# Down as seven products of halves over its first 2048 rows, the other 768 rows plain and late

## The chip, the cores and the metric

The kernel runs on one core of one Trainium2 chip. Its time is the device time of one execution in microseconds (us), and the median over several executions is what is compared. A core has five engines with queues of their own: TensorE (PE in the profile, PEld for its weight loads), VectorE (DVE), ScalarE (ACT), GpSimd (POOL) and SyncE (SP), which here only issues transfers. Transfers are also issued from POOL's queue, among them those that add what they load to what the buffer holds.

## The reference

Two layers of an encoder over 512 tokens and 1024 columns, in float32. Each layer mixes the tokens (attention, pooling and a gated chunk mixing, not touched here) and then applies a SwiGLU block. What the change touches is the last line of the loop:

```python
for l in range(DEPTH):                                   # 2
    ...
    x = x + jnp.einsum('bsn,nd->bsd', mix, w_o[l])
    h = rmsnorm(x, ffn_norm[l])
    g = jnp.einsum('bsd,df->bsf', h, w_gate[l])          # 1024 -> 2816
    u = jnp.einsum('bsd,df->bsf', h, w_up[l])
    x = x + jnp.einsum('bsf,fd->bsd', jax.nn.silu(g) * u, w_down[l])   # 2816 -> 1024: Down
return rmsnorm(x, final_norm)
```

## The kernel before

**Precision.** Each matmul operand is split into two float32r parts, high and low, and a product is three matmuls: high by high, high by low, low by high (`mm3`, line 533; `mm`, line 1243). The high part is a copy on ScalarE, the low part a subtraction on VectorE (or on GpSimd where the engine is `nc.either`). For weights this is `split` (line 560): it writes a `wu` tile of 128 x 2 x 1024, of which there are three. `weights` (line 568) loads a unit of 128 x 1024 into one of two `raw` buffers and splits it. For activations the halves are called `xp`.

**Buffers.** Most things lie in one pool of 32 tiles `u` of 4 KB a partition (`NU`, line 68): activations (`ac`), their halves (`xp`), sums (`xs`), the gated values (`mg`), and the weights of the seven-product stages (`wr`). PSUM has eight banks in three groups, s (3), p (3) and b (2). `anybank` rotates over all of them, `bank("b")` takes one of the two b banks.

**Order.** Nothing is issued where the code stands. `Program` (lines 288 to 490) records every operation, lays out an order by a list scheduler with its own costs, gives out the buffers and then issues all of it from line 488; so every row of the profile names L488, and tiles are told apart by name. An operation that opens a new buffer may be placed at most `lead` matmuls ahead of TensorE (100 in the SwiGLU block, line 1165).

**Gate and up.** They are done as seven products of halves already (Strassen's scheme): tokens, rows and columns are cut in two, and the seven products of sums of quarters are accumulated in six banks, three regions z, y and x of two banks each (`region_banks`, line 1237). The order of the products is 1, 5, 6, 3, 7, 2, 4. The sums of weight quarters are made on VectorE (products 5 and 6 add to a running tile `chain`) or by an adding transfer on POOL's queue (products 7 and 4). The 1408 columns of each half are done in three chunks of 512, 512 and 384 (index c). `consume` (line 1264) turns each result into silu(g) times u and transposes it into `ac` tiles.

**Down in layer 0** (line 1363). A plain product with the weights standing still: 8 output blocks m of 128 columns, each over 22 row blocks k of 128 with all 512 tokens moving, three matmuls each. All 22 halves of the activations (`part`, line 1349) are needed for block 0 already. The result has columns in the partitions, as the residual `res` has; it is added to `res`, scaled into layer 1's input (`scaled`, line 619) and squared for the norm (`squares`, line 629).

**Down in layer 1** (line 1375). The residual is transposed to token rows first (32 transposes). Then the activations stand still: 22 row blocks k, four token tiles, two column halves, into all eight banks; the last three row blocks are kept back, so that the token tiles are finished one after the other, with the final norm and the output.

## Time and profile before

| | |
|---|---|
| median of three runs | 1126.03 us (1125.56 to 1127.54) |
| the profiled execution | 1125.68 us |
| its span, from the first to the last instruction | 1123.8 us |
| mean granted clock of TensorE | 0.991 |
| busy: PE, DVE, ACT, POOL | 1091.9, 781.6, 604.6, 167.9 us |
| Down in layer 0, on TensorE | 440.9 to 562.8 us |
| Down in layer 1, on TensorE | 993.4 to 1113.6 us |

How to read it: a matmul's row in the timeline has the start in us, the length, the operation with output and inputs, and in brackets how long the engine stood idle before it and whose end released it. Matmuls overlap, so a length is longer than the step from one to the next. In a table by windows the columns are busy time and number of instructions of PE, PEld, DVE, ACT and POOL, then the granted clock (1.00 is full speed), the share of the transfer engines' time and GB/s. In a list of groups the two numbers behind the bar are busy time and the mean of one in ns, then idle time before them and who ended it.

### The profile page before, as it was taken

How to read it: one execution, taken by the hardware profiler on the slowest of the kernel's cores; microseconds unless marked ns; L12 is line 12 of the kernel's file. 1: busy time of each engine (PE TensorE's matmuls, PEld its weight loads, DVE VectorE, ACT ScalarE, POOL GpSimd, SP SyncE). 2: the span in 40 equal slices, each digit the busy share in tenths (PEclk: the TensorE clock that was granted, in tenths of full speed). 3: DMA queues.
4: the chain of work that ended last, by engine and by line, in shares of the span. 5: the costliest groups of instructions: out<-in, count | busy, mean ns of one | idle time of the engine just before them, and what ended most of it. 6: DMA issues, size and time to landing. Idle time of an engine off the chain costs nothing.

```text
span 1123.8 us, 14427 instructions
## 1 busy us (share of the span) xinstructions
PE 1091.9 (97%) x5388; PEld 920.2 (82%) x5388; DVE 781.6 (70%) x1107; ACT 604.6 (54%) x949; POOL 167.9 (15%) x187
## 2 busy tenths in 40 slices
PE   9999899999999988999999999999999999999996
PEld 7787788888888987888888877888888889978885
DVE  7679996997786769333336898959976877743324
ACT  6367774775565556222233687747655646642223
POOL 0217320100100111000001363202001100110001
PEclk9999999999999998999999999999999999999998
DMA  6332215456744661333332322165656645533331
GB/s 208 99 117 76 62 57 209 110 148 153 180 101 122 140 151 50 101 94 94 109 101 67 116 62 66 55 241 117 167 167 131 130 119 117 122 94 94 94 113 75
DMA packets 40933, 130.10 MB, mean 116 GB/s; under 512 B 5360, under 2 KB 5616, under 8 KB 40864
## 3 DMA queue, kind: packets, MB, share of 16 engines
q1 hardware_dynamic: 32784, 103.85, 28.7%
q0 software_dynamic: 7504, 24.29, 13.0%
q8 instruction: 42, 0.69, 0.3%
q10 hardware_dynamic: 576, 1.05, 0.2%
q14 instruction: 27, 0.22, 0.1%
HBM read 122.74 MB, written 2.23 MB: 111 GB/s over the span
## 4 chain that ended last, share of the span: by engine, by line
PE 82%; DVE 9%; issue 4%; ACT 3%; POOL 1%; DMA 1%; POOLq 0%; ACTq 0%; DVEq 0%
PE ps L488 82%; DVE u L488 3%; DVE t L488 2%; DVE s L488 1%; DVE wu L488 1%; ACT u L488 1%; ACT t L488 1%; DVE mg L488 1%; ACT wu L488 1%; DVE xp L488 1%; DMA wr<-in_wts 0%; DVE vz L488 0%; DMA u<-u 0%; POOL s L488 0%; ACT vm L488 0%
## 5 line engine op out<-in xcount | busy, mean ns | idle before, releaser
L488 PE MATMUL ps<-wu,xp 128*128 128x512 f32 (+1 forms) x2544 | 555.9, 377 | 3.3 <-ACT wu L488 2.9
L488 PEld LDWEIGHTS ps<-wu,xp 128*128 128x128 f32 x2544 | 466.1, 188 | 76.7 <-ACT wu L488 3.4
L488 DVE TENSOR_TENSOR wu<-wr,wu 128x1024 fp32r<-128x1024 f32 (+1 forms) x168 | 190.4, 1134 | 84.6 <-ACT wu L488 83.7
L488 ACT ACTIVATE wu<-wr 128x1024 fp32r<-128x1024 f32 (+1 forms) x168 | 166.3, 990 | 135.8 <-PE ps L488 109.9
L488 PE MATMUL ps<-u,wu 128*128 128x512 f32 x972 | 236.1, 395 | 2.3 <-DVE wu L488 1.7
L488 PEld LDWEIGHTS ps<-u,wu 128*128 128x128 f32 x972 | 178.9, 188 | 41.8 <-DVE wu L488 3.0
L488 DVE TENSOR_TENSOR wu<-raw,wu 128x1024 fp32r<-128x1024 f32 (+1 forms) x88 | 101.9, 1160 | 153.8 <-ACT wu L488 153.3
L488 ACT ACTIVATE wu<-raw 128x1024 fp32r<-128x1024 f32 (+3 forms) x98 | 97.2, 994 | 201.1 <-PE ps L488 153.2
L488 PE MATMUL ps<-xp,wu 128*128 128x512 f32 x528 | 122.1, 394 | 0.2 <-ACT ac L488 0.2
L488 PEld LDWEIGHTS ps<-xp,wu 128*128 128x128 f32 x528 | 100.6, 191 | 21.7 <-ACT ac L488 0.7
L488 PE MATMUL ps<-u,u 128*128 128x256 f32 (+3 forms) x516 | 107.9, 346 | 4.2 <-ACT t L488 2.6
L488 POOL DMA_DIRECT2D wr<-in_wts x48 | 41.9, 873 | 425.5 <-DVE wr L488 233.4
L488 PEld LDWEIGHTS ps<-u,u 128*128 128x128 f32 (+2 forms) x516 | 75.5, 188 | 18.1 <-ACT t L488 4.2
L488 ACT COPY t<-ps 128x512 f32<-128x512 f32 (+3 forms) x114 | 56.3, 495 | 34.3 <-PE ps L488 30.9
L488 DVE TENSOR_TENSOR u<-ps,u 128x512 fp32r<-128x512 f32 (+1 forms) x104 | 70.0, 684 | 6.1 <-ACT u L488 5.0
L488 ACT ACTIVATE u<-ps 128x512 fp32r<-128x512 f32 (+1 forms) x104 | 61.2, 596 | 16.0 <-PE ps L488 14.7
L488 DVE TENSOR_TENSOR wr<-wr,wr 128x1024 f32<-128x1024 f32 (+1 forms) x48 | 53.9, 1131 | 5.6 <-DMA wr<-in_wts 5.3
L488 ACT ACTIVATE t<-ps,s 128x512 f32<-128x512 f32 x64 | 43.7, 687 | 9.4 <-DVE s L488 7.8
L488 POOL TENSOR_SCALAR t<-t,s 128x512 f32<-128x512 f32 x54 | 37.6, 702 | 66.2 <-DVE s L488 49.7
L488 DVE TENSOR_TENSOR t<-ps,t 64x256 f32<-64x256 f32 (+2 forms) x80 | 42.2, 548 | 5.2 <-ACT t L488 4.8
L488 DVE TENSOR_TENSOR res<-ps,res 128x512 f32<-128x512 f32 x40 | 27.5, 688 | 25.3 <-PE ps L488 25.1
L488 DVE TENSOR_REDUCE s<-ps 128x1 f32<-128x512 f32 x64 | 42.4, 679 | 0.8 <-PE ps L488 0.6
(128 smaller groups left out, 845.3 us busy)
## 6 DMA issues: line engine op xcount, KB each, us to landing
raw<-in_wts SPq DMA_DIRECT2D x82, 512.0 KB, 3.5
wr<-in_wts SPq DMA_DIRECT2D x64, 512.0 KB, 4.8
wr<-in_wts POOLq DMA_DIRECT2D x32, 512.0 KB, 5.6
wr<-in_wts SPq DMA_DIRECT2D x32, 384.0 KB, 3.4
wr<-in_wts POOLq DMA_DIRECT2D x16, 384.0 KB, 5.5
u<-u SPq DMA_DIRECT2D x32, 128.0 KB, 2.3
raw<-in_wts SPq DMA_DIRECT2D x8, 320.0 KB, 3.0
res<-in_xT SPq DMA_DIRECT2D x8, 256.0 KB, 5.2
```

Source lines behind the costliest of these rows:

```text
L488: getattr(getattr(nc, op.engine), op.method)(*[real(x) for x in op.args], **{k: real(x) for k, x in op.kw.items()})
```

## The change

Down of both layers becomes one piece of code. Its first 16 row blocks (those of chunks 0 and 1, eight of each half of F) are done as seven products of halves: two halves of the tokens, two halves of the rows, two halves of the columns. The last six row blocks (chunk 2) are done plainly (`rest`), once for each half of the columns, and late: for columns 512 to 1023 between products 7 and 4, for columns 0 to 511 after product 4. The order is product 1, product 5, products 6 and 3 block by block in turn, 2, 7, late part 1, 4, late part 0. The weights are packed to match (34 loads of 512 KB for a layer instead of 22, eight of them adding transfers); `consume` now transposes each token tile of chunks 0 and 1 by itself, into tiles by quarter. In layer 0, too, the result now has tokens in the partitions: `back` transposes it, 32 transposes in all, and adds it to `res`. Since columns 512 to 1023 are finished first, layer 1 takes its input blocks in the order 4 to 7, 0 to 3. The splits of the products' weights name VectorE, those of the late part leave the engine open.

The core of the diff:

```diff
-        KORDER = range(KD)
+        KORDER = range(KD) if l == 0 else (4, 5, 6, 7, 0, 1, 2, 3)
...
-        if not last:
...
-                for k in range(KF):
...
-                    xh, xl = part(k)
-                    mm3(ps[:], w[:, 0, s], w[:, 1, s], xh, xl, k == 0, k == KF - 1)
+        def back(y, t, s):
+            ps = bank("b")
+            for m in range(4):
+                nc.tensor.transpose(ps[:, m * P : (m + 1) * P], y[:, m * P : (m + 1) * P], ident[:])
+            nc.vector.tensor_tensor(out=rows(t, s), in0=cols4(ps[:]), in1=rows(t, s), op=ALU.add)
...
+        def halved(src):
+            hi, lo = (upool.tile([P, 4, HALF], F32R, tag="u", name=nm("xp"), bufs=NU) for _ in range(2))
+            nc.scalar.activation(flat(hi), flat(src), AF.Copy)
+            add(flat(lo), flat(src), f32(flat(hi)), ALU.subtract)
+            return hi, lo
...
+            if p == 5:
+                sums[c] = upool.tile([P, 4, HALF], F32, tag="u", name=nm("xs"), bufs=NU)
+                add(flat(sums[c]), flat(x21), flat(x22), ALU.subtract)
+                add(flat(x21), flat(x11), flat(x21), ALU.subtract)
+            elif p == 6:
+                add(flat(sums[c]), flat(sums[c]), flat(x11), ALU.subtract)
+            else:
+                add(flat(sums[c]), flat(sums[c]), flat(x12))
...
+            if p == 1:
+                chain[b] = fetch(l, dn_unit(0, 0, b))
+                return chain[b]
+            if p == 2:
+                return fetch(l, dn_unit(1, 0, b))
+            if p == 4:
+                add_loaded(l, chain[b], dn_unit(1, 0, b))
+                return chain[b]
+            if p == 7:
+                raw = fetch(l, dn_unit(0, 1, b))
+                add_loaded(l, raw, dn_unit(1, 1, b))
+                return raw
+            if p == 3:
+                return chain["22"]
+            raw = fetch(l, dn_unit(0, 1, b) if p == 5 else dn_unit(1, 1, b))
+            chain["22"] = raw
+            add(chain[b][:], chain[b][:], raw[:])
+            return chain[b]
...
+        def products(ps_):
+            xs = {}
+            for b in range(4):
+                for p in ps_:
+                    if b % 2 == 0:
+                        xs[p] = halved(sum_of(p, b // 2))
+                    xh, xl = xs[p]
+                    wu = split(operand(p, b), U, nc.vector)
+                    for j in range(2):
+                        for kk in range(2):
...
+        def rest(h, targets, after):
+            wus = [weights(l, dn_unit(2, h, b)) for b in range(3)]
+            for i, (banks, opens) in enumerate(targets):
+                for j in range(2):
+                    for k in range(6):
...
+        products([1])
...
+        products([5])
...
+        products([6, 3])
...
+        products([2])
+        products([7])
+        spare = [bank("b"), bank("b")]
...
+        rest(1, [(reg["y"], False), (spare, True)], after1)
+        products([4])
+        if not last:
+            next_inputs(1)
...
+        rest(0, [(reg["x"], False), (reg["z"], False)], after0)
+        if not last:
+            next_inputs(0)
+            xg = nxt
```

Where the instructions come to stand is shown at three places. The first is TensorE's queue at the end of up in layer 0. Before, the last up product (128x384) is followed by the transposes of the gated values `mg` of chunk 2, and then by the first matmuls of Down (`ps_4088`, output block 0):

```order
L488 MATMUL ps_3759<-wu_3984,xp_2454 128x384
L488 MATMUL ps_3759<-wu_3984,xp_2333 128x384 x2
L488 MATMUL ps_3759<-wu_3984,xp_2454 128x384
L488 MATMUL ps_4058<-ident,mg_3716 128x128 x4
L488 MATMUL ps_4065<-ident,mg_3716 128x128 x2
L488 MATMUL ps_4073<-ident,mg_3740 128x128 x4
L488 MATMUL ps_4078<-ident,mg_3740 128x128 x2
L488 MATMUL ps_4088<-xp_3900,wu_4006 128x512
```

Now the first matmuls of product 1 (`ps_4067` and `ps_4082`, region z; `wu_4015` is its first weight block) stand directly behind up:

```order
L493 MATMUL ps_3759<-wu_3987,xp_2333 128x384 x2
L493 MATMUL ps_3759<-wu_3987,xp_2454 128x384
L493 MATMUL ps_4067<-wu_4015,xp_3898 128x512 x2
L493 MATMUL ps_4071<-ident,mg_3740 128x128
L493 MATMUL ps_4073<-ident,mg_3740 128x128
L493 MATMUL ps_4067<-wu_4015,xp_3934 128x512
L493 MATMUL ps_4067<-wu_4015,xp_3898 128x512 x2
L493 MATMUL ps_4067<-wu_4015,xp_3934 128x512
L493 MATMUL ps_4082<-wu_4015,xp_3898 128x512 x2
L493 MATMUL ps_4071<-ident,mg_3740 128x128 x3
L493 MATMUL ps_4073<-ident,mg_3740 128x128
```

Two groups of transposes of `mg_3740` have moved in among the matmuls of the first product; those of `mg_3716` stand further ahead, among up's.

The second place is VectorE's queue in layer 0 while TensorE begins Down. Before (`xp` from `ac` are the halves of the activations, `wu` from `raw` a split):

```order
L488 TENSOR_TENSOR xp_4103<-ac_3340,xp_3976 128x1024
L488 TENSOR_TENSOR xp_4112<-ac_3439,xp_4017 128x1024
L488 TENSOR_TENSOR xp_4119<-ac_3445,xp_3992 128x1024
L488 TENSOR_TENSOR xp_4126<-ac_4001,xp_4041 128x1024
L488 TENSOR_TENSOR wu_4086<-raw_4046,wu_4086 128x1024
L488 TENSOR_TENSOR xp_4141<-ac_4052,xp_4062 128x512
L488 TENSOR_TENSOR xp_4148<-ac_4069,xp_4095 128x1024
L488 TENSOR_TENSOR xp_4155<-ac_4071,xp_4106 128x512
L488 TENSOR_TENSOR wu_4129<-raw_4084,wu_4129 128x1024
L488 TENSOR_TENSOR wu_4165<-raw_4143,wu_4165 128x1024
```

Now, in products 1 and 5 (`wr` from `wr,wr` is a sum of weight quarters, `xs` one of activations):

```order
L493 TENSOR_TENSOR wu_4075<-wr_3941,wu_4075 128x1024
L493 TENSOR_TENSOR wr_3900<-wr_3900,wr_3975 128x1024
L493 TENSOR_TENSOR xp_4104<-xs_4049,xp_4064 128x1024
L493 TENSOR_TENSOR wu_4100<-wr_3990,wu_4100 128x1024
L493 TENSOR_TENSOR wr_3912<-wr_3912,wr_4008 128x1024
L493 TENSOR_TENSOR wu_4119<-wr_3900,wu_4119 128x1024
L493 TENSOR_TENSOR wr_3941<-wr_3941,wr_4019 128x1024
L493 TENSOR_TENSOR xs_4141<-ac_3477,ac_3383 128x1024
L493 TENSOR_TENSOR wu_4136<-wr_3912,wu_4136 128x1024
L493 TENSOR_TENSOR wr_3990<-wr_3990,wr_4047 128x1024
L493 TENSOR_TENSOR wu_4161<-wr_3941,wu_4161 128x1024
```

Between two splits stand one or two sums that were not there.

The third place is TensorE in layer 0 in late part 1 (`ps_4158` and `ps_4170` are region y, `ps_4631` the first spare bank, `t` the finished token rows). Before, output blocks followed each other with nothing between them; now transposes stand between:

```order
L493 MATMUL ps_4170<-wu_4587,xp_4448 128x512 x2
L493 MATMUL ps_4170<-wu_4587,xp_4500 128x512
L493 MATMUL ps_4619<-ident,t_4362 128x128 x4
L493 MATMUL ps_4626<-ident,t_4395 128x128 x4
L493 MATMUL ps_4631<-wu_4533,xp_4412 128x512 x2
L493 MATMUL ps_4631<-wu_4533,xp_4451 128x512
L493 MATMUL ps_4631<-wu_4533,xp_4412 128x512 x2
```

The transposes of `t_4395` stand two rows behind the last matmul into the bank that it is made from.

More of the change, by code (lines that the diff above doesn't have):

```diff
@@ L1276, in consume @@
                     )
+                    if c < 2:
+                        if (i, s, c) not in act:
+                            act[i, s, c] = upool.tile([P, 4, HALF], F32, tag="u", name=nm("ac"), bufs=NU)
+                        ps = bank("b")
+                        for f in range(nf):
+                            fs = slice(f * P, (f + 1) * P)
+                            nc.tensor.transpose(ps[:, fs], stash[i, s][:, j, fs], ident[:])
+                        nc.scalar.copy(
+                            out=act[i, s, c][:, :, j * P : (j + 1) * P], in_=ps[:].rearrange("p (f q) -> p f q", q=P)
+                        )
+                        return
                     if j == 0:
@@ L1343, in encoder @@
                             consume(z, j, 1, 0)
[L1346 to L1383 removed]
+        if last:
+            for m in range(KD):
+                ps = bank("b")
                 for t in range(NT):
@@ new lines, in encoder, with next_inputs, add @@
+        settle = finish if last else back
+        nxt = [None] * KD
+        if not last:
+            acc = tpool.tile([P, T], F32, tag="acc", name=nm("acc"), bufs=2)
+        def next_inputs(s):
+            for m in range(4 * s, 4 * s + 4):
+                nxt[m] = scaled(m, (l + 1) * NCOL + m)
+                squares(res[:, m], acc, not started)
+                started.append(m)
+        started = []
+        def add(out_, a, b, op=ALU.add):
+            nc.vector.tensor_tensor(out=out_, in0=a, in1=b, op=op)
@@ new lines, in halved, with sum_of @@
+        def halved(src):
[3 more added lines that the diff above has]
+            return hi, lo
+        sums = [None, None]
+        def sum_of(p, c):
+            x11, x21, x12, x22 = (act[i, s, c] for s in range(2) for i in range(2))
+            if p == 1:
+                return x11
+            if p == 2:
+                return x12
+            if p == 4:
+                return x22
+            if p == 7:
+                return x21
+            if p == 5:
[6 more added lines that the diff above has]
+                add(flat(sums[c]), flat(sums[c]), flat(x12))
+            return sums[c]
@@ new lines, in encoder, with rest_part @@
+        KREST = [(s, f) for s in (1, 0) for f in range(3)]
+        rest_parts = {}
+        def rest_part(n):
+            s, f = KREST[n]
+            g = s, f // 2
+            if g not in rest_parts:
+                m = U if f // 2 == 0 else T
+                hi, lo = (upool.tile([P, 2, T], F32R, tag="u", name=nm("xp"), bufs=NU) for _ in range(2))
+                nc.scalar.activation(flat(hi)[:, :m], flat(act[g])[:, :m], AF.Copy)
+                add(flat(lo)[:, :m], flat(act[g])[:, :m], f32(flat(hi)[:, :m]), ALU.subtract)
+                rest_parts[g] = hi, lo
+            return [x[:, f % 2] for x in rest_parts[g]]
@@ new lines, in encoder, with kept @@
+        a1, u1, v5 = {}, {}, {}
+        def kept(ps, t, s, sign):
+            y = tmp()
+            if last:
+                add(cols4(y[:]), cols4(ps), rows(t, s), sign)
+            else:
+                nc.scalar.copy(out=y[:], in_=ps)
+            return y
+        products([1])
+        for j in range(2):
+            a1[j] = kept(reg["z"][j][:], j, 0, ALU.add)
+        products([5])
+        for j in range(2):
+            v5[j] = tmp()
+            nc.scalar.copy(out=v5[j][:], in_=reg["y"][j][:])
@@ new lines, in encoder, with after1 @@
+        products([6, 3])
+        for j in range(2):
+            u1[j] = kept(reg["z"][j][:], j, 1, ALU.subtract)
+        products([2])
+        products([7])
+        spare = [bank("b"), bank("b")]
+        def after1(i, j):
+            y = v5[j] if i else u1[j]
+            if i == 0:
+                add(y[:], reg["y"][j][:], y[:], ALU.subtract)
+            else:
+                add(y[:], spare[j][:], y[:])
+                if last:
+                    add(cols4(y[:]), cols4(y[:]), rows(2 + j, 1))
+            settle(y, 2 * i + j, 1)
@@ new lines, in encoder, with after0 @@
+        for j in range(2):
+            add(v5[j][:], v5[j][:], reg["z"][j][:], ALU.subtract)
+        rest(1, [(reg["y"], False), (spare, True)], after1)
+        products([4])
+        if not last:
+            next_inputs(1)
+        def after0(i, j):
+            if i == 0:
+                y = a1[j]
+                add(y[:], reg["x"][j][:], y[:])
+            else:
+                y = tmp()
+                if last:
+                    add(cols4(y[:]), cols4(reg["z"][j][:]), rows(2 + j, 0))
+                else:
+                    nc.scalar.copy(out=y[:], in_=reg["z"][j][:])
+            settle(y, 2 * i + j, 0)
@@ L1441, in encoder @@
+        rest(0, [(reg["x"], False), (reg["z"], False)], after0)
+        if not last:
+            next_inputs(0)
+            xg = nxt
         nc.lead = LEAD
```

147 lines of the change are left out of this document (62 added, 85 removed).

## The prediction

> **What bounds the kernel now.** I read the page first (span, chain of waits, instruction groups), then the busy time by stage, then the timeline of TensorE around the stage that changes. One execution is followed: span 1123.8 us, its time 1125.68 us, so 1.9 us lie outside the span; the median of the three runs is 1126.03 us, 0.35 above it. The sum below is made against 1125.68.
>
> ```profile
> span 1123.8 us, 14427 instructions
> PE 82%; DVE 9%; issue 4%; ACT 3%; POOL 1%; DMA 1%; POOLq 0%; ACTq 0%; DVEq 0%
> ```
>
> The chain that ended last runs for 82% of the span over TensorE (PE). The stages (columns: window, then busy time of PE, its weight loads, DVE, ACT, POOL, then clock, DMA share, GB/s) say where TensorE is alone on it. The first two rows lie in the first chunk of gate in layer 0, the other two in Down of layers 0 and 1.
>
> ```profile
> 210.00:225.00 15.00, 15.00 (x72) 12.52 (x71) 14.16 (x15) 10.98 (x15) 3.26 (x3) 1.00 0.52 144
> 240.00:255.00 15.00, 15.00 (x67) 12.28 (x66) 14.92 (x20) 10.21 (x13) 1.72 (x2) 1.00 0.35 71
> 441.00:560.00 119.00, 119.00 (x516) 98.36 (x517) 47.86 (x52) 33.58 (x41) 1.06 (x2) 0.98 0.31 94
> 1010.00:1101.00 91.00, 91.00 (x403) 75.19 (x402) 29.41 (x26) 24.77 (x25) 0.00 (x0) 1.00 0.31 93
> ```
>
> In Down TensorE never stops, and VectorE (DVE) is busy 40% of layer 0's and 32% of layer 1's window. So a matmul less in Down is time less, and there is room beside it. The first two rows show how far that room goes: in gate, which has been made of seven products all along, VectorE is full (14.92 of 15.00 us) and TensorE still had no gap.
>
> **The price of a matmul.** From the timeline of TensorE (start, length, instructions):
>
> ```profile
> 329.66 22.38 PE L488 MATMUL ps<-wu,xp 128*128 128x512 f32 x98
> 351.88 0.40 PE L488 MATMUL ps<-ident,mg 128*128 128x128 f32 x2
> 440.90 122.08 PE L488 MATMUL ps<-xp,wu 128*128 128x512 f32 x528 [0.25 <-ACT ac L488]
> 562.82 12.40 PE L488 MATMUL ps<-u,wu 128*128 128x512 f32 x54
> 993.38 120.20 PE L488 MATMUL ps<-wu,xp 128*128 128x512 f32 x528
> ```
>
> An undisturbed run of 98 takes 351.88 - 329.66 = 22.22 us, 0.2267 us each; Down of layer 1 gives 120.20 / 528 = 0.2277. Which operand stands still makes no difference. Plain Down is 22 k-blocks x 8 output blocks x 3 terms = 528 matmuls a layer. The change does 16 of the 22 k-blocks as 7 products x 8 k x 2 token tiles x 3 = 336, and 6 plainly: 6 x 8 x 3 = 144. That is 480, 48 less a layer: 96 x 0.2267 = **-21.8 us**.
>
> **Turning back.** Layer 0 now gets its output with tokens in the rows and turns it back with 32 transposes that it did not need. Four in a row take 653.85 - 653.49 = 0.36 us:
>
> ```profile
> 653.49 0.60 PE L488 MATMUL ps<-ident,t 128*128 128x128 f32 x4
> 653.85 1.18 PE L488 MATMUL ps<-u,u 96*128 96x512 f32 x4
> ```
>
> 8 x 0.36 = **+2.9 us**, all on TensorE. Layer 1 had its 32 transposes of res before and keeps them.
>
> **The gaps ahead of Down.** TensorE's idle time and who ended it, and the clock in 4 us steps around the gaps:
>
> ```profile
> 410.60 0.61 PE L488 MATMUL ps<-wu,xp 128*128 128x384 f32 x2 [2.90 <-ACT wu L488]
> 411.59 11.23 PE L488 MATMUL ps<-wu,xp 128*128 128x384 f32 x55 [0.38 <-DVE wu L488]
> 438.89 1.76 PE L488 MATMUL ps<-ident,mg 128*128 128x128 f32 x6 [2.71 <-DVE mg L488]
> 985.92 0.65 PE L488 MATMUL ps<-ident,mg 128*128 128x128 f32 x4 [1.81 <-DVE mg L488]
> 989.86 0.41 PE L488 MATMUL ps<-ident,mg 128*128 128x128 f32 x2 [0.55 <-ACT res L488]
> ```
>
> ```profile
> 412.00:416.00 4.00, 4.00 (x17) 4.00 (x17) 1.59 (x3) 1.23 (x2) 1.56 (x2) 0.66 0.96 238
> 440.00:444.00 4.00, 3.75 (x11) 2.75 (x10) 4.00 (x5) 3.38 (x5) 0.00 (x0) 0.50 0.02 6
> 444.00:448.00 4.00, 4.00 (x16) 3.21 (x15) 4.00 (x5) 0.00 (x0) 0.00 (x0) 0.82 0.00 0
> 985.00:990.00 5.00, 3.54 (x24) 3.30 (x24) 5.00 (x4) 1.65 (x4) 3.10 (x2) 1.00 0.49 134
> ```
>
> Plain Down needs the last chunk's activations early, so TensorE stands until VectorE has them (mg): 2.71 + 0.25 us in layer 0, 1.81 + 0.55 in layer 1. After the longer gap the clock is 0.50 and 0.82 for 4 us each, which loses 4 x 0.50 + 4 x 0.18 = 2.7 us; by count it is 121.92 - 528 x 0.2267 = 2.2. I take 2.3. VectorE was late there because GpSimd did two weight subtractions (2.7 us each) beside it, and its own instructions swelled to 3.29:
>
> ```profile
> 431.63 3.29 DVE L488 SCALAR_TENSOR_TENSOR mg<-t,rs,mg 128x384 f32<-128x384 f32 x2
> 431.69 5.44 POOL L488 TENSOR_TENSOR wu<-raw,wu 128x1024 fp32r<-128x1024 f32 x2 [17.89 <-ACT wu L488]
> ```
>
> Now the first product needs only chunk 0, the last chunk is used much later, and the new splits are VectorE's alone. The gaps go with their slow clock: -(2.96 + 2.3) - 2.36 = **-7.6 us**. What is late next is the wait of the two or three transposes that still stand among the first product's matmuls; it is in the next term. The gap at 410.60 belongs to gate/up, its fetches keep their order, and it stays.
>
> **VectorE in the first products.** Its new work per layer: 28 splits instead of 16, 8 weight sums, 8 activation sums, 14 subtractions for the halves. Its step, from two neighbours in the timeline, is 214.50 - 213.36 = 1.14 us; the other rows are ScalarE's (ACT) part of a split, the evictions and the scalings of layer 1's inputs (mean ns after the comma):
>
> ```profile
> 213.36 1.22 DVE L488 TENSOR_TENSOR wu<-wr,wu 128x1024 fp32r<-128x1024 f32 x1
> 214.50 1.22 DVE L488 TENSOR_TENSOR xs<-xq,xq 128x1024 f32<-128x1024 f32 x1
> L488 ACT ACTIVATE wu<-wr 128x1024 fp32r<-128x1024 f32 x112 | 118.9, 1062 | 96.1 <-PE ps L488 74.3 <-DVE wr L488 11.7 <-issue 4.8
> L488 DVE TENSOR_TENSOR t<-ps,t 128x512 f32<-128x512 f32 x32 | 20.6, 682 | 0.0
> L488 ACT COPY res<-ps 128x512 f32<-128x512 f32 x8 | 4.3, 621 | 2.6 <-PE ps L488 2.6
> L488 ACT ACTIVATE u<-res,colt 128x512 fp32r<-128x512 f32 x16 | 11.5, 716 | 16.9 <-DVE res L488 15.9 <-DMA res<-in_xT 1.0
> L488 DVE SCALAR_TENSOR_TENSOR u<-res,colt,u 128x512 fp32r<-128x512 f32 x16 | 11.9, 749 | 5.8 <-ACT u L488 5.8
> ```
>
> A weight block feeds 12 matmuls, 2.72 us. In VectorE's new order 22 instructions of layer 0 lie from the one behind the first product's first split to the first split of product 6: 20 x 1.14 and two of 384 columns at some 0.6 (a 512-wide one takes 0.68), 24.0 us, beside products 1 and 5, 8 x 2.72 = 21.8 us. Only three wu buffers let it run ahead, so TensorE waits about 2 us there, in pieces of 1 to 1.5 with the wait for the last transposes. From there to the last split of product 3 the two are even (15 x 1.14 = 17.1 beside 7 x 2.72 = 19.0). ScalarE, at 1.06 a split, is not full. Layer 0: **+2.0 us** (0 if VectorE comes in 2.2 us ahead, as the gate rows suggest it can; 3.8 if it sets the pace, below). In layer 1 the 32 transposes of res now lie inside product 1 and give VectorE 2.9 us, but they pass through the two b banks and not all eight: each pair waits for two copies of 0.62 us, 1.24 against 0.72 of transposing, four times, **+2.3 us** (0.5 to 4).
>
> **Late rows and hand-overs.** In layer 0's first late part (for columns 512 to 1023) two transposes must follow VectorE's additions (0.68 us and a hand-over of some 0.2 on each side, as in the first row of the tail, below: 1.1), and the spare banks open only when res has been added from them: I count 0.7 + 0.3 + 1.1 = **+2.1 us** (0 to 4). The late part holds all three wu buffers, so each hand-over to the next product waits for a split, 1.06 + 1.14 us with 12 matmuls (2.72 us) over it: nearly hidden, I take **+1.0 us** for both layers. The start of layer 1 begins with blocks 4 to 7, which are ready; they have 4 x 3 x 2 = 24 matmuls in the two pool projections, 5.4 us, and these cover the copy, four transposes, the last addition and the two scalings of block 0 (0.62 + 0.36 + 0.68 + 0.72 + 0.75, with four hand-overs 3.9 us): nothing.
>
> **The tail.** The end of the last three token tiles that are finished, from the addition of the residual to the scaling:
>
> ```profile
> 1101.37 0.69 DVE L488 TENSOR_TENSOR t<-ps,res 128x512 f32<-128x512 f32 x1 [0.23 <-PE ps L488]
> 1110.84 0.68 DVE L488 TENSOR_TENSOR t<-ps,res 128x512 f32<-128x512 f32 x1
> 1113.58 0.72 ACT L488 ACTIVATE t<-t,s 128x512 f32<-128x512 f32 x1 [1.23 <-POOL s L488]
> 1114.05 0.69 DVE L488 TENSOR_TENSOR t<-ps,res 128x512 f32<-128x512 f32 x1
> 1114.99 1.26 POOL L488 TENSOR_TENSOR t<-t,fint 128x512 f32<-128x512 f32 x1 [1.45 <-ACT t L488]
> 1117.30 0.72 ACT L488 ACTIVATE t<-t,s 128x512 f32<-128x512 f32 x1 [1.75 <-POOL s L488]
> ```
>
> The last token tile needed 1117.30 - 1114.05 = 3.25 us from addition to scaling, the one before it 2.74, since GpSimd's product with fint and the first half's square were in the way. Both are gone: **-0.5 us**.
>
> **Sum.** -21.8 + 2.9 - 7.6 + 2.0 + 2.3 + 2.1 + 1.0 - 0.5 = -19.6; 1125.7 - 19.6 = **1106 us**. With all four waits at zero it is 1098.7.
>
> **Rivals.** (a) The gap ahead of Down stays in another form, since the transposes of the last chunk still stand early in TensorE's order: 1106 + 7.6 = 1114. Against it: between them and the stop lie other matmuls, and GpSimd is out. Chance 0.12. (b) VectorE sets the pace. A block of product 5 asks 3 steps (3.42 against 2.72 us), a pair of 6 and 3 five (5.70 against 5.44): 4 x 0.70 + 4 x 0.26 = 3.8 a layer, 7.7 instead of 4.3; and if the clock falls twice a layer in these gaps, 4 x 2.7 more: 1106 + 3.4 + 10.8 = 1120. For it speaks the step count, against it the gate rows above, and that a gap of 1.81 us left the clock at 1.00. Chance 0.13. The Trainium skill ("TensorE: Matmul & The Clock Gate", A second HAM failure mode: psum-queue depth-cycling) says that frequent short idle times between groups of matmuls make the clock oscillate; by that rule (b) would be the likely case. The trace here had its fall after 2.71 us and none after 1.81, so I leave it the minor one.
>
> (c) Slower: weights come late. Each of the 32 buffers is fetched into only when something frees it, and the change adds 12 fetches and 8 adding DMAs a layer. It has happened once:
>
> ```profile
> 408.65 1.86 DVE L488 TENSOR_TENSOR wr<-wr,wr 128x768 f32<-128x768 f32 x2 [5.27 <-DMA wr<-in_wts]
> wr<-in_wts SPq DMA_DIRECT2D x64, 512.0 KB, 4.8
> wr<-in_wts POOLq DMA_DIRECT2D x32, 512.0 KB, 5.6
> ```
>
> It cost 2.90 + 0.38 us and 4 x 0.34 of clock, 4.6 us. From the fifth such stop the change loses: 1106 + 5 x 4.6 = 1129. Against it: in layer 0's new order 115 to 133 matmuls lie between the reader that frees the buffer and the first use of the block, for products 5 and 6; that is 26 us or more, against 4.8 to 5.6 us of landing. Chance 0.06; 0.02 for a gain that cancels to within 0.2%.
>
> **The numbers.** The forecast has 0.67. Faster by over 0.2% (2.3 us, about what a measurement of this kernel can tell): 0.67 + 0.12 + 0.13 = 0.92; same 0.02; slower 0.06. The range of 8 in 10 goes from 1099 (no new wait) to 1118: that takes in (a) and half of (b), and leaves out the rest of (b), (c) and the lower edge.
>
> **What would show it.** In the new trace: 64 matmuls fewer (96 off, 32 on); no gap of over 1 us before Down's first product and a clock of 1.00 there; TensorE's waits on VectorE's wu in products 5 to 3 of about 2 us in layer 0, on ScalarE's res copies in product 1 of layer 1; the gap near 408 unchanged. I am wrong if VectorE's idle time in the products is ended by DMA, if the clock falls inside them, or if Down takes over 113 us in either layer.

## The result, and the profile after

The changed kernel takes 1097.23 us, median of four runs (1096.46 to 1098.71), beside 1125.94 us for the kernel before: 0.9744 of it, 95% interval 0.9727 to 0.9761. Two later measurements beside other experiments gave 0.9775 (0.9754 to 0.9795; 1099.94 us) and 0.9773 (0.9757 to 0.9789; 1099.36 us). So the change saves 25 to 29 us. The forecast was 1106, with a range down to 1099: faster, as said, but by more than said; the two later measurements lie at the lower end of the range, the first below it.

The page of the kernel after, its span and the chain that ended last (shares of the span):

```profile
span 1094.7 us, 14521 instructions
PE 84%; DVE 8%; issue 4%; ACT 3%; DMA 1%; POOL 1%; POOLq 0%; DVEq 0%; ACTq 0%
```

The profiled execution took 1096.46 us, 1.8 of it outside the span. TensorE holds two hundredths more of the chain than before; nothing has replaced it. The timeline of TensorE (start, length, instructions) from the stop near 410 us through Down of layer 0:

```profile
409.92 0.62 PE L493 MATMUL ps<-wu,xp 128*128 128x384 f32 x2 [2.00 <-ACT wu L493]
410.92 11.29 PE L493 MATMUL ps<-wu,xp 128*128 128x384 f32 x55 [0.37 <-DVE wu L493]
...
435.70 1.62 PE L493 MATMUL ps<-wu,xp 128*128 128x512 f32 x6
437.16 0.60 PE L493 MATMUL ps<-ident,mg 128*128 128x128 f32 x4
437.51 72.03 PE L493 MATMUL ps<-wu,xp 128*128 128x512 f32 x316
509.39 0.60 PE L493 MATMUL ps<-ident,t 128*128 128x128 f32 x4
510.33 0.66 PE L493 MATMUL ps<-ident,t 128*128 128x128 f32 x4 [0.35 <-DVE t L493]
...
516.09 0.66 PE L493 MATMUL ps<-ident,t 128*128 128x128 f32 x4 [0.79 <-DVE t L493]
...
550.14 1.30 PE L493 MATMUL ps<-u,wu 128*128 128x512 f32 x5
```

Down follows the last matmul of up without a gap. From 437.51 on it runs 71.9 us without a stop, through products 1, 5, 6 and 3, 2 and 7, where the forecast had 2 us of waits for VectorE and more at the hand-overs. The only stops, 0.35 and 0.79 us, are those of the transposes that turn the late rows back. (A few matmul records are missing, so the counts are a little low.) The same view in layer 1:

```profile
975.77 0.95 PE L493 MATMUL ps<-wu,xp 128*128 128x512 f32 x3
976.59 1.09 PE L493 MATMUL ps<-ident,res 128*128 128x128 f32 x8
977.43 0.72 PE L493 MATMUL ps<-wu,xp 128*128 128x512 f32 x2
977.99 1.08 PE L493 MATMUL ps<-ident,res 128*128 128x128 f32 x8
978.82 2.31 PE L493 MATMUL ps<-wu,xp 128*128 128x512 f32 x9
980.97 1.03 PE L493 MATMUL ps<-ident,res 128*128 128x128 f32 x8
981.76 0.72 PE L493 MATMUL ps<-wu,xp 128*128 128x512 f32 x2
982.31 1.08 PE L493 MATMUL ps<-ident,res 128*128 128x128 f32 x8
983.14 103.85 PE L493 MATMUL ps<-wu,xp 128*128 128x512 f32 x456
```

The transposes of res go in groups of eight, two banks at a time, and the order puts matmuls of product 1 between the groups; ScalarE's copies run under these. No row has an idle time. Then 103.85 us to the end.

Where the 29 us of the profiled execution come from is read by laying marks in the two timelines: the same instruction in both, and the difference between one mark and the next. Each row runs from the mark of the row above to its own. The columns before and after have the time of the mark in us, the column forecast the prediction's terms for that stretch, the last one the measured difference.

| to this mark | before | after | forecast | measured |
|---|---|---|---|---|
| end of the stop near 410 us (from the start) | 410.60 | 409.92 | 0 | -0.7 |
| first matmul of Down, layer 0 | 440.90 | 435.70 | -3.0 | -4.5 |
| first matmul of layer 1 | 562.82 | 550.14 | -5.7 | -7.5 |
| first four vm transposes | 678.15 | 666.23 | 0 | +0.8 |
| first eight t transposes in a row | 727.36 | 714.17 | 0 | -1.3 |
| first mg transposes of the last chunk, layer 1 | 973.45 | 960.29 | 0 | 0.0 |
| end of the last matmul | 1113.57 | 1086.99 | -10.4 | -13.4 |
| end of the span | 1123.8 | 1094.7 | -0.5 | -2.5 |
| sum | | | -19.6 | -29.1 |

The second profile of the kernel after has the marks 411.85, 437.71, 553.19, 669.25, 717.20, 963.39, 1090.11 and a span of 1097.8: the same differences to the kernel before within 0.1 us, but for the first (+1.3) and Down of layer 0 (-6.4), which differ from execution to execution. The -1.3 us in the middle of layer 1 is chance too: the kernel before had its clock down there, the first row below, and no other profile of this study had it but that of the kernel with all 22 blocks (0.66 as well). The second row is the same place, after the same stops, in the kernel after.

```profile
680.00:685.00 5.00, 4.61 (x24) 4.26 (x23) 3.62 (x8) 3.23 (x8) 2.15 (x3) 0.66 0.89 225
```

```profile
670.00:675.00 5.00, 5.00 (x31) 4.12 (x32) 4.02 (x8) 3.69 (x7) 2.55 (x3) 1.00 0.79 253
```

### The profile page after: what moved, and what is told of

It reads as the page before. It is cut to its first block, busy times and chain, and to the rows that moved or that the text cites. A ratio compares the mean times of both kernels' runs of the same rounds, so it can differ in the third digit from the quotient of the medians.

```text
span 1094.7 us, 14521 instructions
## 1 busy us (share of the span) xinstructions
PE 1070.3 (98%) x5324; PEld 900.6 (82%) x5324; DVE 864.6 (79%) x1196; ACT 648.8 (59%) x995; POOL 170.5 (16%) x198
## 4 chain that ended last, share of the span: by engine, by line
PE 84%; DVE 8%; issue 4%; ACT 3%; DMA 1%; POOL 1%; POOLq 0%; DVEq 0%; ACTq 0%
PE ps L493 84%; DVE u L493 4%; DVE t L493 2%; DVE s L493 1%; ACT u L493 1%; ACT t L493 1%; DVE wu L493 1%; ACT wu L493 1%; DMA wr<-in_wts 0%; DVE vz L493 0%; DMA u<-u 0%; ACT vm L493 0%; DVE z L493 0%; POOL u L493 0%; POOL r L493 0%
## 5 line engine op out<-in xcount | busy, mean ns | idle before, releaser
L493 PE MATMUL ps<-wu,xp 128*128 128x512 f32 (+1 forms) x2976 | 658.7, 380 | 2.4 <-ACT wu L493 2.0
L493 PEld LDWEIGHTS ps<-wu,xp 128*128 128x128 f32 x2976 | 547.0, 188 | 93.0 <-ACT wu L493 2.3
L493 ACT ACTIVATE wu<-wr 128x1024 fp32r<-128x1024 f32 (+1 forms) x224 | 225.3, 1008 | 200.1 <-PE ps L493 162.6
L493 DVE TENSOR_TENSOR wu<-wr,wu 128x1024 fp32r<-128x1024 f32 (+1 forms) x224 | 258.3, 1156 | 92.2 <-ACT wu L493 91.4
L493 ACT ACTIVATE wu<-raw 128x1024 fp32r<-128x1024 f32 (+3 forms) x66 | 63.1, 959 | 65.1 <-PE ps L493 40.0
L493 DVE TENSOR_TENSOR wu<-raw,wu 128x1024 fp32r<-128x1024 f32 (+3 forms) x60 | 67.6, 1130 | 27.1 <-ACT wu L493 26.6
L493 DVE TENSOR_TENSOR wr<-wr,wr 128x1024 f32<-128x1024 f32 (+1 forms) x64 | 73.7, 1154 | 4.8 <-DMA wr<-in_wts 4.4
L493 DVE TENSOR_TENSOR t<-ps,t 128x512 f32<-128x512 f32 (+2 forms) x92 | 50.4, 567 | 20.7 <-PE ps L493 16.2
L493 PE MATMUL ps<-ident,t 128*128 128x128 f32 x288 | 43.7, 274 | 4.0 <-DVE t L493 2.1
L493 PEld LDWEIGHTS ps<-ident,t 128*128 128x128 f32 x288 | 34.0, 140 | 15.1 <-issue 5.0
```

What stands on the lines that cost most here:

```text
L493: getattr(getattr(nc, op.engine), op.method)(*[real(x) for x in op.args], **{k: real(x) for k, x in op.kw.items()})
```

## The experiments

The theory after the result: a part of the gain is Strassen's matmuls, as forecast; a part is that Down's weight subtractions no longer go to GpSimd; and of the four waits that the forecast counted at 7.4 us, those on VectorE and on the transposes of res are not there, since VectorE starts early enough and the order puts matmuls between. The rival: the extra gain belongs to the execution (clock, landing of transfers), or VectorE has real room and was never near its limit.

**One layer at a time.** The new code for one layer, the old for the other (`l in NEW` chooses in Down, in the layout of the activations and in the packing of the weights).

```diff
+NEW = (0,)        # the other kernel: (1,)
-                    if c < 2:
+                    if c < 2 and l in NEW:
```

> Layer 0 with the seven products, layer 1 with the plain Down of the kernel before. By the accounting of the two traces (start of Down 5.2 us earlier with four transposes moved behind it, Down itself 7.5 us shorter, the later start and middle of layer 1 about 0.9 us better): 1126 - 13 = 1113 us, or 1114 if the clock's fall near 680 us in layer 1 of the kernel before comes back here. By the terms of the prediction (half of the matmuls -10.9, back transposes +2.9, gap and clock -5.3, waits +4.6): 1117. If the gain of the whole does not come from the layers one by one (alignment, a lucky clock), the two layers alone do not add up to it.

> Layer 1 with the seven products, layer 0 with the plain Down. By the accounting of the two traces (13.4 us in layer 1 from the gap ahead of Down to the last matmul, 2.5 us behind it): 1126 - 16 = 1110 us, 1111.6 if the 1.6 us between the last output packet and the end do not belong to the change. By the terms of the prediction (-10.9 -2.4 +2.3 +0.5 -0.5): 1115.

Measured beside a kernel before of 1124.78 us: layer 0 alone 1112.05 (ratio 0.9891, 0.9876 to 0.9906), layer 1 alone 1110.13 (0.9868, 0.9854 to 0.9883). That is -12.7 and -14.7, together -27.4: the layers add up, and each has about the value of the accounting, not that of the forecast's terms (-8.7 and -11.0). In layer 0's kernel the end of the program, with the old code, took 7.9 us from the last matmul to the end, where the kernel before has 10.2; so 2.3 of its 12.7 us lie there, and most of the -2.5 us at the end is not the change's. The other 10.4 or so are still more than the 8.7 of the terms.

**The engine of the subtractions.** Plain Down as before, but VectorE does all its weight subtractions.

```diff
-                        w = weights(l, 74 + blk // 8)
+                        w = weights(l, 74 + blk // 8, nc.vector)
-                w = weights(l, 74 + k)
+                w = weights(l, 74 + k, nc.vector)
```

> The kernel before, with every weight subtraction of Down on VectorE and none on GpSimd. If VectorE was late ahead of Down because GpSimd's two subtractions ran beside it (its pair of mg took 3.29 us instead of 1.14), the gap in layer 0 falls from 2.7 us to under 1, the clock stays at 1.00, and with the 1.8 us in layer 1 the time falls by 5 to 8 us: 1119. If the gap lies in plain Down's need of the last chunk, it stays, and VectorE has two more steps ahead of it: 1125 to 1128.

Measured beside 1124.78: 1116.55 us, ratio 0.9931 (0.9915 to 0.9948): -8.2 us with two words added and no matmul saved. By the same marks its profile has 2.7 us less ahead of Down in layer 0, 2.1 less in it, and 2.9 less in layer 1 from the last chunk's transposes to the last matmul, 7.6 in all. TensorE at the start of plain Down in layer 0, this kernel:

```profile
434.74 0.88 PE L488 MATMUL ps<-ident,mg 128*128 128x128 f32 x6
436.15 0.87 PE L488 MATMUL ps<-ident,mg 128*128 128x128 f32 x6 [0.53 <-ACT ac L488]
437.48 12.77 PE L488 MATMUL ps<-xp,wu 128*128 128x512 f32 x55 [0.46 <-ACT ac L488]
```

The stop of 2.71 us for VectorE's mg is gone; what is left is 0.53 and 0.46 for ScalarE's copies, and the clock stays at 1.00. The opposite edit, the kernel after with the planner free to use GpSimd in the products:

```diff
-                    wu = split(operand(p, b), U, nc.vector)
+                    wu = split(operand(p, b), U)
```

> The kernel after, where the planner may again give weight subtractions of the products to GpSimd; it gives it two, one in each layer. If the engine choice was worth its 8 us through the gap ahead of plain Down alone, it is worth little here, since the first product doesn't need the last chunk: 0 to 2 us from the steps of VectorE that swell beside GpSimd, 1097 to 1099 beside 1126. If GpSimd beside VectorE costs TensorE wherever it stands, or short of VectorE the products stop: 1102 to 1105. If a step less on VectorE, which is at its edge, helps: 1095 to 1096.

Measured beside 1124.46: 1102.14 us, ratio 0.9796 (0.9773 to 0.9818), 2 to 6 us slower than the kernel after. This interval overlaps with those of the two later measurements of the kernel after, so the time alone doesn't settle it; the rows do. With one subtraction a layer on GpSimd the stop is back in both layers. TensorE, then VectorE and GpSimd in layer 0:

```profile
435.36 0.66 PE L493 MATMUL ps<-ident,mg 128*128 128x128 f32 x4 [1.80 <-DVE mg L493]
...
975.70 0.66 PE L493 MATMUL ps<-ident,mg 128*128 128x128 f32 x4 [1.80 <-DVE mg L493]
```

```profile
432.06 3.25 DVE L493 SCALAR_TENSOR_TENSOR mg<-t,rs,mg 128x384 f32<-128x384 f32 x2
```

```profile
432.44 2.44 POOL L493 TENSOR_TENSOR wu<-wr,wu 128x1024 fp32r<-128x1024 f32 x1 [18.36 <-ACT wu L493]
```

The same pair on VectorE in the kernel after, and its first split for Down and its first for product 6:

```profile
431.24 1.14 DVE L493 SCALAR_TENSOR_TENSOR mg<-t,rs,mg 128x384 f32<-128x384 f32 x2
432.29 1.22 DVE L493 TENSOR_TENSOR wu<-wr,wu 128x1024 fp32r<-128x1024 f32 x1
...
456.25 1.22 DVE L493 TENSOR_TENSOR wu<-wr,wu 128x1024 fp32r<-128x1024 f32 x1
```

The pair of mg takes 3.25 us beside GpSimd's 2.44 and 1.14 without: VectorE loses 2.1 us, and TensorE stops for 1.80, though the first product needs only chunk 0. The transposes of the last chunk stand ahead of it in TensorE's order. The Trainium skill ("SBUF — State Buffer", SBUF: two separate sides) says that a VectorE instruction with two inputs in SBUF and a GpSimd instruction that reads SBUF exclude each other: the one that starts second waits for the whole of the first; the 2.1 us lost beside a GpSimd instruction of 2.44 agree with that.

**How near VectorE is to its limit.** It does the subtraction of product 5's four blocks twice; nothing else changes.

```diff
                     wu = split(operand(p, b), U, nc.vector)
+                    if p == 5:
+                        nc.vector.tensor_tensor(out=wu[:, 1], in0=chain[b][:], in1=f32(wu[:, 0]), op=ALU.subtract)
```

> The kernel after, with VectorE doing the subtraction of each of product 5's weight blocks twice: 4 steps of 1.14 us more in each layer, and TensorE's work as before. In the trace of after the first split for product 6 in layer 0 was ready about 0.5 us before TensorE reached it, and some in product 6/3 less. If VectorE is at that edge, nearly all of it shows: 4 x 1.14 - 0.5 = 4.1 us in layer 0 and 2 to 4 in layer 1, 1103 to 1105 us. If VectorE has real room (its busy share is 77% of layer 0's Down), nothing: 1097. If short stops also lower the clock, 3 us a layer more: 1109 and above.

Measured beside 1124.78: 1106.38 us, ratio 0.9838 (0.9821 to 0.9855), 7 to 11 us slower than the kernel after. Its profiled execution has Down of layer 0 at 119.6 us (114.4 in the kernel after) and of layer 1 at 116.7 (113.0). TensorE in layer 0:

```profile
453.17 2.56 PE L493 MATMUL ps<-wu,xp 128*128 128x512 f32 x10 [0.40 <-DVE xp L493]
456.57 3.05 PE L493 MATMUL ps<-wu,xp 128*128 128x512 f32 x12 [0.84 <-DVE wu L493]
461.11 11.23 PE L493 MATMUL ps<-wu,xp 128*128 128x512 f32 x48 [1.49 <-DVE wu L493]
472.95 40.67 PE L493 MATMUL ps<-wu,xp 128*128 128x512 f32 x178 [0.61 <-DVE wu L493]
```

```profile
460.00:464.00 4.00, 2.89 (x13) 2.31 (x14) 4.00 (x4) 3.82 (x6) 0.00 (x0) 1.00 0.00 0
```

Nearly all of the 4 x 1.14 = 4.6 us a layer comes out as time: Down is 5.2 us longer in layer 0 (3.8 to 4.1 against the later profiles of the kernel after) and 3.7 in layer 1, and the stops begin in product 5 itself. VectorE in the kernel after is at its limit, and only just ahead. The rival that it has real room falls. The clock stays at 1.00 in this execution through four stops in 20 us. By the Trainium skill ("TensorE: Matmul & The Clock Gate", A second HAM failure mode: psum-queue depth-cycling) frequent short idle times make the clock oscillate; at this size this trace does not show it.

**The price of a matmul.** Each matmul of product 2 twice, 48 more a layer.

```diff
+                            for again in range(2 if p == 2 else 1):
-                                p in OPENS and k == 0, k == 7,
+                                    p in OPENS and k == 0 and again == 0, k == 7,
```

> The kernel after, with every matmul of product 2 done twice: 48 more in each layer, as many as the change takes out, with no more weights and no more VectorE work (the sums of this product are wrong by that). If TensorE paces Down all through, 96 x 0.2267 = 21.8 us: 1119 us beside 1126, 1118 beside 1124.8. If a part of the gain came from work that has now more room (VectorE behind product 2, the late rows), less, 18 to 20; if the matmuls were not what the change saved, well below that.

Measured beside 1124.46: 1119.48 us, ratio 0.9953 (0.9937 to 0.9968), 20 to 24 us above the kernel after. Down grows to 125.4 us in layer 0 and 124.3 in layer 1, by 11.0 and 11.3: 0.23 us a matmul. TensorE sets the pace of Down all through.

**Turning back, and the transposes of res.** Two kernels, each without one set of 32 transposes: layer 0's `back` adds the unturned rows, and layer 1 leaves out the loop that turns res with its copies.

```diff
-            ps = bank("b")
-            for m in range(4):
-                nc.tensor.transpose(ps[:, m * P : (m + 1) * P], y[:, m * P : (m + 1) * P], ident[:])
-            nc.vector.tensor_tensor(out=rows(t, s), in0=cols4(ps[:]), in1=rows(t, s), op=ALU.add)
+            nc.vector.tensor_tensor(out=rows(t, s), in0=cols4(y[:]), in1=rows(t, s), op=ALU.add)
```

> The kernel after without layer 0's 32 transposes that turn the output back (the token rows are added to the residual unturned, which leaves that part of the computation out). By the prediction's price of a transpose, 32 x 0.09 = 2.9 us less, 0.9974 of the kernel after. By the trace of after, in which layer 0's Down takes 114.4 us instead of the 111.6 of its matmuls and transposes and stops twice for 1.1 us: 2.9 + 1.1 and part of another 1.6, 4 to 5.6 us less. If the transposes fill time that TensorE would otherwise wait: nothing.

> The kernel after without layer 1's 32 transposes of res inside product 1 and their 8 copies (the residual is then added unturned, so that part of the computation is left out). If they pass through their two banks without stopping TensorE, as its trace shows, they cost 32 x 0.09 = 2.9 us and it is that much faster than after. If they hold TensorE up as the prediction has it, 2.9 + 2.3 = 5.2 us. If their time gives VectorE the room that it needs in product 5, part of it comes back as stops there: 1 to 2 us.

Without turning back: 1091.92 us beside a kernel after of 1099.94 on the same chip, ratio to before 0.9705 (0.969 to 0.972), -8.0 us, more than any expectation. TensorE in Down of layer 0 has no stop left:

```profile
438.55 107.78 PE L493 MATMUL ps<-wu,xp 128*128 128x512 f32 x472
```

In the profiles, Down of layer 0 falls from 115.5 to 109.4 us and the start of layer 1 by 0.5, and the stop near 410 us ends 1.0 earlier, which isn't its doing: 6.6 us are the transposes' own. That is 2.9 of transposing and 3.7 of what comes with it; 1.6 of the 3.7 are stops that the profile beside it shows in the late rows (0.42 behind ScalarE, 0.35 and 0.79 behind VectorE), the rest was not taken apart. Without the transposes of res: 1095.72 beside a kernel after of 1099.36, ratio 0.9743 (0.9725 to 0.9761), -3.6 us; its stretch from the first matmul of Down in layer 1 to the last falls by 2.4 us (113.3 to 110.9). TensorE in that stretch:

```profile
976.78 26.50 PE L493 MATMUL ps<-wu,xp 128*128 128x512 f32 x114
1003.50 0.74 PE L493 MATMUL ps<-wu,xp 128*128 128x512 f32 x2 [0.21 <-ACT wu L493]
1004.80 81.07 PE L493 MATMUL ps<-wu,xp 128*128 128x512 f32 x356 [0.57 <-DVE wu L493]
```

So the 32 transposes cost about their own 2.9 us and no wait that a row shows; 0.8 us come back as stops, as VectorE is now the later one. The other 1.2 of the 3.6 us lie in layer 0, which the edit leaves as it was. The forecast's 5.2 falls.

**Weights in time.** Two kernels for the transfers: one large buffer fewer, and fetches let in 130 matmuls ahead instead of 100 (`NU = 31`; `LEAD_FF = 130`).

> The kernel after with 31 of the large buffers instead of 32. If fetches have room in Down (26 us from the buffer's release to its use, against 4.5 to 5.6 of landing) nothing stops there: at most the stop near 410 us grows by some 1 us, 1096 to 1098. If the weights in Down come only just in time (the third rival of the prediction), stops of 1 to 3 us in each layer: 1100 and above.

> The kernel after, with fetches of the feed-forward part let in 130 matmuls ahead of their use instead of 100. If the stop of TensorE near 410 us (2.0 and 0.4 us, and some 1.7 us of lower clock behind it) comes from a fetch that the order lets in too late, it goes: 1093. If it comes from the buffers, which are freed no earlier, nothing changes: 1097, or more where a buffer taken early is missed elsewhere.

With 31 buffers: 1108.35 us, ratio 0.9854 (0.9836 to 0.9873), 8.4 above the kernel after on the same chip. TensorE and ScalarE in layer 0's late rows:

```profile
509.84 0.96 PE L493 MATMUL ps<-wu,xp 128*128 128x512 f32 x3 [2.97 <-ACT wu L493]
```

```profile
501.46 1.06 ACT L493 ACTIVATE wu<-raw 128x1024 fp32r<-128x1024 f32 x1 [0.71 <-PE ps L493]
508.73 1.06 ACT L493 ACTIVATE wu<-raw 128x1024 fp32r<-128x1024 f32 x1 [6.20 <-DMA raw<-in_wts]
```

The third block of plain weights comes through a pair of small buffers (raw), so its fetch starts only when VectorE has done with the first. The kernel after has the same wait at the same place. In its first profile ScalarE waits 4.87 us for that transfer, TensorE doesn't stop, and Down takes 114.4 us; in its third 6.05, TensorE stops for 0.78, and Down takes 115.8. ScalarE in the first, then ScalarE and TensorE in the third:

```profile
504.63 1.06 ACT L493 ACTIVATE wu<-raw 128x1024 fp32r<-128x1024 f32 x1 [4.87 <-DMA raw<-in_wts]
```

```profile
506.98 1.06 ACT L493 ACTIVATE wu<-raw 128x1024 fp32r<-128x1024 f32 x1 [6.05 <-DMA raw<-in_wts]
```

```profile
508.09 3.81 PE L493 MATMUL ps<-wu,xp 128*128 128x512 f32 x15 [0.78 <-ACT wu L493]
```

So weights come just in time here, and there is no room left on that side. What else the missing buffer costs is spread over Down (120.2 us in layer 0, 115.1 in layer 1) and was not taken apart. Fetching earlier doesn't help: 1101.00 us, ratio 0.979 (0.9775 to 0.9804), with the stop near 410 us as long (2.36 and 0.38) and Down of layer 1 at 115.3 us. Which buffer holds up the fetch near 410 us is left open.

**More blocks in the products.** 20 of the 22 k-blocks in the seven products, and the plain rows of tokens 0 to 255 ahead of product 4; then all 22, with product 4's last three blocks done for one half of its tokens after the other. The layout of the activations and the packing of the weights change to match. The core of the first:

```diff
-            for b in range(4):
+            for b in range(5):
...
-        products([4])
-        if not last:
-            next_inputs(1)
-        rest(0, [(reg["x"], False), (reg["z"], False)], after0)
+        rest(0, [(0, reg["x"], False)], after0)
+        products([4])
+        if not last:
+            next_inputs(1)
+        rest(0, [(1, reg["z"], False)], after0)
```

> The kernel after with 20 of the 22 k-blocks of 128 rows in the seven products and 2 plain, and the plain rows of tokens 0 to 255 ahead of product 4. 7 x 10 x 2 x 3 + 2 x 8 x 3 = 468 matmuls a layer instead of 480: -24 x 0.2267 = -5.4 us. VectorE has a quarter more work in the products, but product 1, in which it has only one step for 12 matmuls, is longer too, so it keeps its lead; the last tiles come 1.4 us apart instead of 4.1, which may cost 1 us at the end. 1092 to 1093 beside 1126 (1091 to 1092 beside 1124.8). If VectorE, at its edge in the kernel after, falls behind: the 5.4 us are lost again, 1097 to 1100.

> The kernel after with all 22 k-blocks in the seven products, no plain rows, and the last three weight blocks of product 4 done for one half of its tokens after the other: 7 x 11 x 2 x 3 = 462 matmuls a layer instead of 480, -36 x 0.2267 = -8.2 us against the kernel after, 1088 to 1089 beside 1126. With 20 blocks 3.7 of 5.4 us came, the rest went into one stop of 1.5 us behind ScalarE and an end 1 us longer; if that happens again in both layers: 1091 to 1092.

> The kernel with 20 of 22 k-blocks in the seven products, beside the kernel after on one chip. By 24 matmuls fewer 5.4 us less than after; by its first trace (one stop of 1.5 us in layer 1, an end 1 us longer, no stop in layer 0's late rows) 4 to 7 less, 1091 to 1094. If its first result came from the chip it ran on: within 2 us of after.

The kernel after was measured again beside these and the kernels without transposes, since chips differ by about a microsecond:

> The kernel after once more, so that the runs beside it can be compared with it on one chip: 0.9744 of the kernel before. It also gives a second profile: if the fall of the clock near 680 us in the kernel before was chance, none there again; if the stop near 410 us belongs to the kernel, it is there with some 2 us.

> The kernel after a third time, to stand beside the next two on one chip. Its first two measurements gave 0.9744 and 0.9775 of the kernel before; between those two by either theory, 1097 to 1100.

It gave 1099.94 and 1099.36 us, as told with the result, with the stop near 410 us at 2.69 and 3.13 us and no fall of the clock in the middle of layer 1.

20 blocks: 1092.19 us, ratio 0.9711 (0.9694 to 0.9729), and on another chip 1093.46 (0.9720, 0.9706 to 0.9733) beside a kernel after of 1099.36: -5.9 us, about the 5.4 of its 24 matmuls. Of the kernels that leave nothing out it is the fastest. With one block of plain weights instead of three, TensorE in Down of layer 0 has no stop left up to the late rows, nor in them:

```profile
435.66 83.09 PE L493 MATMUL ps<-wu,xp 128*128 128x512 f32 x364
```

The layers share the gain unevenly. By the profiles of the second measurement, Down takes 109.7 us in layer 0 and 112.3 in layer 1, where the kernel after beside it has 115.8 and 113.3. Each layer has 2.7 us of matmuls less; layer 0 gains 3.4 more, with the stops of its late rows gone, while layer 1 gains only 1.0, and the end is 1.0 longer. In layer 1 TensorE now stops once behind ScalarE, in both profiles; in the first:

```profile
1017.42 62.39 PE L493 MATMUL ps<-wu,xp 128*128 128x512 f32 x272 [1.49 <-ACT wu L493]
```

All 22 blocks: 1099.99 us, ratio 0.9778 (0.9761 to 0.9794), the same as the kernel after beside it (1099.94). Down of layer 0 is at 109.9 us as with 20 blocks, but layer 1's takes 118.9 instead of 112.4. TensorE there:

```profile
1013.07 16.61 PE L493 MATMUL ps<-wu,xp 128*128 128x512 f32 x72 [0.35 <-DVE wu L493]
1030.18 4.81 PE L493 MATMUL ps<-wu,xp 128*128 128x512 f32 x18 [0.49 <-DVE xp L493]
1035.69 0.73 PE L493 MATMUL ps<-wu,xp 128*128 128x512 f32 x2 [0.70 <-ACT wu L493]
1036.95 30.86 PE L493 MATMUL ps<-wu,xp 128*128 128x512 f32 x126 [0.53 <-DVE wu L493]
1069.00 0.73 PE L493 MATMUL ps<-wu,xp 128*128 128x512 f32 x2 [1.20 <-ACT wu L493]
1070.45 3.92 PE L493 MATMUL ps<-wu,xp 128*128 128x512 f32 x16 [0.72 <-DVE wu L493]
1076.02 15.27 PE L493 MATMUL ps<-wu,xp 128*128 128x512 f32 x66 [1.65 <-DVE t L493]
```

Seven stops, 5.6 us, behind VectorE and ScalarE; behind the fourth the clock is at 0.80 and 0.77 for 4 us each, which loses 1.7 us more. Here the saved matmuls turn into waits.

## Why the prediction was right in kind and short in size

- **The matmuls, -21.8 us: right.** Doubling 48 a layer adds 22.3 us to Down.
- **The gaps ahead of Down, -7.6 us: right in size, half right in reason.** Moving the subtractions to VectorE alone gives -8.2 us. But the prediction gave two reasons, that the first product needs only chunk 0 and that GpSimd is out; with GpSimd back a stop of 1.80 us is back in both layers, so the first alone does not remove the gap, and rival (a) was one engine choice away. In layer 0 one thing was missed: the six transposes between the gap and Down ran at the low clock, 440.90 - 438.89 - 0.25 = 1.8 us, where the same six in the kernel before with its subtractions on VectorE took 437.48 - 436.15 - 0.46 = 0.9. That 0.9, the four transposes (0.36) that now lie behind the mark, and 0.3 that was not taken apart make the -4.5 instead of -3.0 in the table.
- **VectorE in the first products, +2.0 us: absent. This is the step that failed first.** The 22 instructions behind the first split, up to and with that of product 6, took the 24.0 us that were counted (the split of product 6 begins 22.8 us after the first split's end and takes 1.14), but the count let VectorE and TensorE start together. VectorE starts on Down's weights 3.4 us before Down does (432.29 against 435.70), between its last instructions for up, and has its first split done 2.3 us ahead. So it is ahead by about half a microsecond when TensorE comes to product 6 at 435.70 + 0.36 + 96 x 0.2275 = 457.9. The bracket of the prediction, 0 if VectorE comes in 2.2 us ahead, is what happened; the sum took the other value.
- **Res through two banks, +2.3 us: absent.** (Four times 1.24 - 0.72 is 2.1, not 2.3.) The step took the groups of transposes as if they stood in a row. TensorE's order has product 1's matmuls between them, and their removal gives 2.4 us in the stretch, close to 2.9 less the 0.8 that return. This could have been read in the order before the run.
- **Hand-overs, +1.0 us: absent**; no row shows them in either layer.
- **Late rows and turning back, +2.1 and +2.9 us: short by 0.6 to 1.6.** Removing both gives 6.6 us against the second profile, and 5.6 against the first, whose Down of layer 0 was 1.0 shorter. Part of the 6.6 is the wait for the third block of plain weights (0.42 there, 0.78 in the third profile), which the prediction did not see.
- **The tail, -0.5 us: right for the part it named** (from the last addition to the last scaling 3.25 us before, 1089.77 - 1087.03 = 2.74 after). The last addition also starts 0.04 us behind the last matmul instead of 0.48, since VectorE is free by then. Another 1.6 us lie behind the last scaling, below.
- **Weights late, the third rival at 0.06: it did not decide, but it was far nearer than it was given.** The prediction counted 26 us from a buffer's release to its use for products 5 and 6 and did not count the plain weights' small pair, where ScalarE waits for a transfer in all three profiles of the kernel after.

Of the prediction's own signs, the 64 matmuls fewer, the missing gap ahead of Down and the stop near 410 us came; the waits for VectorE's splits and for the copies of res did not. Its sign of being wrong, Down over 113 us in either layer, came as well (114.4 in layer 0, 113.0 in layer 1), but it did not fit the sum: with the forecast's terms Down of layer 0 would take 121.9 - 5.7 = 116.2 us.

By the table: 5.3 us of absent waits, 1.2 around the gap ahead of Down in layer 0 and 2.0 at the tail, with 2.0 of chance in this execution (the first stretch and the clock in layer 1), are 10.5; 0.8 at the start of layer 1 and 0.2 elsewhere go the other way, which leaves the 9.5 between -19.6 and -29.1. Against the later measurements (25.1 and 25.4 us saved) the forecast is short by 5.5 to 5.8. That the time lies near 1098.7, the prediction's sum without any new wait, is partly luck: the late rows did stop, and what the tail and the low clock gave, which the sum did not have, made up for it.

## What to carry to other kernels

When work moves to another engine, lay its instructions and the reader's against each other from the point at which each may start, not from a common one, and look into the order for what stands between two steps before pricing a wait. Of 25 to 29 us here, 8 could be had without the algorithm, by keeping one engine's subtractions out of the other's way: test the incidental part of a change by itself. A saving of matmuls is worth its price only as far as the engines and buffers that feed them have room: 20 blocks brought the price of their matmuls in the sum of both layers, 22 nothing against the kernel after.

## What the runs showed of the hardware

- The clock falls after some stops and not after others of the same length. At the stop near 410 us it fell in most profiles (here the kernel after, after 2.00 us; with fetches let in earlier 2.36 us brought it to 0.63), while in the one with VectorE's doubled steps 2.39 us left it at 1.00, and in the first of 20 blocks 2.27. Shorter stops in a row differ in the same way: 1.34, 0.36, 0.99 and 0.40 us within 8 us stand ahead of the 0.66 near 680 us in the kernel before, and the same four, within 0.02 us, left it at 1.00 in the kernel after. The Trainium skill ("TensorE: Matmul & The Clock Gate", What's actually happening) describes an activity window that runs free of the program; that the same stop has different outcomes agrees with it. In the same section the Trainium skill has the clock fall after an idle window of about 3.4 us; here a stop of 2.00 us was enough.

```profile
412.00:416.00 4.00, 4.00 (x19) 4.00 (x19) 1.53 (x2) 1.33 (x2) 0.89 (x2) 0.73 0.84 127
```

- The program's end depends on more than its last instruction. In the kernel before the last output lands 3.7 us before the span's end, and in between one packet of the instruction queue is seen, the row below (packets, MB, share), 2.5 us before the end; in the kernel after the last output lands 2.2 us before the end and there is no such packet. The kernel before with its subtractions on VectorE has the packet and 3.4 us, the one with the new layer 0 and the old end has none behind its last output and 1.4 us. Over all profiles, those without a packet behind the last output take 1.4 to 2.7 us there. That the packet costs the 1.5 us is argued from the order of events, not shown by a run.

```profile
q14 instruction: 1, 0.01, 2.0%
```
